# Cross-covariance attention on one core: one late store cut into seven parts instead of four

## The chip, the cores and the metric

The kernel runs on one core of one Trainium2 chip. The metric is device time in microseconds of one execution. Before the change three runs took 128.46 us at the median (128.16 to 128.62). A measurement of this kernel can tell differences of about 0.3% (0.4 us).

## The reference

For each of 8 x 12 = 96 heads, Q, K and V are 512 x 64 in float32. Attention runs over the 64 features and not over the 512 positions:

```
Q_norm = Q / (norm over the 512 positions)      # per feature
K_norm = K / (norm over the 512 positions)
attn = softmax(Q_norm^T K_norm, last axis)      # 64 x 64 for each head
out  = V attn                                   # 512 x 64
```

Inputs and output are 12.58 MB each, so that 37.75 MB are read and 12.58 MB written.

## The kernel before, in words

**Tiling.** Four heads make a unit (`HU` = 4), two units a step (`S` = 12 steps), two steps a group of V (`W` = 6). For a unit, Q and K arrive as 128 partitions x 16 rows of 64; DVE casts them side by side to bfloat16 (L212); PE multiplies each 32 x 128 piece by itself, so that one 128 x 128 sum holds q.q, q.k and k.k (`grams`, L232). The diagonals give the norms (`squares`, `sums`, `powers`), the q.k block is scaled, transposed (`logits`), exponentiated with its row sum (`exps`, L281) and divided (`normalise`, L290). V is cast, transposed by PE (`vtrans`, L301) and copied to SBUF (`vcopy`). `outs` (L318) multiplies it by the normalised weights; `ocopy` copies each quarter of a step's output from PSUM into a tile `so`. When two quarters are there, `store(s, i)` writes the tile to `out`: 128 partitions x 2 runs (the index r = 0 or 1) of 2 KB each, 512 KB. There are 24 such stores, two a step, and 13 buffers for `so`.

**Order of the work.** The order on each engine is fixed when the program is built. A planner (`Order`) is given every piece of work with its engine, its cost, what it needs and a rank, and lists the pieces in order of their planned begin. Loads and stores are pieces of an engine "DMA" and go to SP's queue in the planned order (ACT issues two of the first loads). The plan gives each store one cost and does not look at how `store` divides it, so the diff moves no other piece.

**The end of SP's queue.** After the last loads of V (L196), SP issues the last stores: fourteen whole ones (L206; the last of them is called S14 here), then the divided store FEW = (S - 3, 1), the second half of step 9, and then four whole ones of steps 10 and 11 (L206; T1 to T4 here). FEW leaves in four DMAs: its first half (r = 0) in partitions 0 to 91, 92 to 99 and 100 to 127 (L203, here P1 to P3), and its second half (r = 1) whole (L204, P4). FEW has the same 256 runs of 2 KB as every other store, of which the 92 + 8 + 28 parts hold 128 and P4 the other 128.

**Eight semaphores in turn.** The framework gives the DMAs on the hardware queues eight completion semaphores in turn (DMAHW0 to DMAHW7), and an issue waits until the DMA that had its semaphore before, eight DMAs earlier, has landed. SP executes its list in order, so that while one issue waits, the ones behind it wait too. The ends of the two lists, with the waits, stand in the section on the change.

Of the kernel before, what the change touches and what calls it, by code (L numbers as in the profile page):

```python
# [102 lines left out]
def kernel(  # L103
# [7 lines left out]
    nc = tc.nc  # L111
# [50 lines left out]
    qk32, v32, vb, qkb, gram, scr, kq, n2, r8, kqs, rq, lg, ex, ab, vps, vt, po, so = ({} for _ in range(18))  # L162
# [35 lines left out]
    def store(s, i):  # L198
        o = Of[s // 2, s % 2, i].rearrange("p r (j d) -> p r j d", d=D)
        if (s, i) == FEW:  # L200

            for a, b in ((0, 92), (92, 100), (100, 128)):
                nc.sync.dma_start(out=o[a:b, 0], in_=so[s, i][a:b, 0])  # L203
            nc.sync.dma_start(out=o[:, 1], in_=so[s, i][:, 1])  # L204
            return
        nc.sync.dma_start(out=o, in_=so[s, i])  # L206

# [139 lines left out]
    for i in range(NB["ab"]):  # L347
        a = const.tile([128, HU, 2 * D], BF16, name=f"ab{i}")
# [42 lines left out]
    for u in range(U):  # L391
        s, r = divmod(u, 2)
# [21 lines left out]
    for w in range(W):  # L414
        both = 2 * w >= BOTH
        for r in range(2):
            halves = (0, 1) if (w, r) == (W - 1, 1) else (None,)
            n = 2 * w + r - NB["v"]
# [22 lines left out]
    for s in range(S):  # L441
        for x in range(4):
            i, k = divmod(x, 2)
            n = 4 * s + x - 2
            wait = [("oc", n // 4, n % 4)] if n >= 0 else []
            order = [("ou", s, x - 1) if x else back("ou", s, 1, 3)]
            piece(("ou", s, x), {"PE": 0.5}, [("vc", s // 2, *t) for t in turns(s // 2) if t[0] // 2 == k] + [("nm", s)] + wait, order, R["ou"] + 0.01 * s, outs, s, x)
            n = 2 * s + i - NB["so"]
            free = [("st", n // 2, n % 2)] if k == 0 and n >= 0 else []
            order = [("oc", s, x - 1) if x else back("oc", s, 1, 3)]  # L450
            piece(("oc", s, x), {"ACT": 0.6, "DVE": (0.68, BIAS["oc"])} if s >= BOTH else {"ACT": 0.6}, [("ou", s, x)] + free, order, R["oc"] + 0.01 * s, ocopy, s, x)
        for i in range(2):
            order = [("st", s, 0) if i else back("st", s, 1, 1)]
            piece(("st", s, i), {"DMA": X}, [("oc", s, 2 * i), ("oc", s, 2 * i + 1)], order, v_at(2 * s + i) + ST_LAG, store, s, i)
# [43 lines left out]
```

## Time and profile before

| | |
|---|---|
| median of 3 runs | 128.46 us |
| the profiled execution: its time | 128.35 us |
| the profiled execution: span from first to last instruction | 126.5 us |
| busy: DVE, PE, ACT, POOL | 72%, 62%, 57%, 30% of the span |
| DMA: mean rate over the span | 400 GB/s |
| start of the last compute instruction (ACT copies `so`, L166) | about 115 us |
| issue of the last store | 119.66 us |

How to read it: the span is the profiled execution's own, and its time of 128.35 us has 1.8 us more around it. Every change in the span is set against 128.35 us, which lies 0.11 us under the median of the runs. The "DMA" columns of the profile are a mean over the core's 16 DMA engines. A share a little over 1 occurs, because the records of consecutive packets on one engine overlap by a few ns.

### The profile page before, as it was taken

What the parts mean: (1) busy time and instruction counts of PE and PEld (TensorE: products, weight loads), DVE (VectorE), ACT (ScalarE), POOL (GpSimd) and SP (SyncE); (2) the same over time, 40 slices, a digit from 0 to 9 for tenths busy, and PEclk for the clock granted to TensorE, in tenths of its full rate; (3) what the DMA queues carried; (4) which work ended last, traced back from release to release, by engine and by line L of the source; (5) the groups of instructions that cost most, each with busy time, mean ns of one, the idle gap of its engine ahead of it and who ended that gap; (6) DMA issues with size and microseconds to landing.
All of it is one profiled execution on the core that took longest, in us unless ns stands there. A gap on an engine that the chain in (4) does not pass through costs nothing.

```text
span 126.5 us, 4885 instructions
## 1 busy us (share of the span) xinstructions
PE 78.9 (62%) x2128; PEld 64.2 (51%) x2128; DVE 90.7 (72%) x141; ACT 72.5 (57%) x220; POOL 37.4 (30%) x40
## 2 busy tenths in 40 slices
PE   0065393895964679958583999596676858473000
PEld 0054382784843568747372788484464746352000
DVE  3344749839899499899976798999999799740000
ACT  4000441539789077695883688694758969974000
POOL 4006307300745913043064303133363270300000
PEclk9999999999599555899998559959999999855555
DMA  3999999999999999999999999999999999999993
GB/s 129 408 434 411 427 413 421 413 434 408 430 417 418 409 422 417 398 414 425 422 417 412 418 419 421 416 423 423 401 415 411 402 401 407 400 407 408 405 382 149
DMA packets 15359, 50.64 MB, mean 400 GB/s; under 512 B 1130, under 2 KB 1130, under 8 KB 13930
## 3 DMA queue, kind: packets, MB, share of 16 engines
q1 hardware_dynamic: 15050, 49.29, 96.5%
q10 hardware_dynamic: 288, 1.05, 2.1%
q8 instruction: 16, 0.26, 0.7%
q14 instruction: 5, 0.04, 0.1%
HBM read 37.75 MB, written 12.58 MB: 398 GB/s over the span
## 4 chain that ended last, share of the span: by engine, by line
DVE 34%; DMA 21%; PE 19%; ACT 10%; issue 5%; POOL 2%; SPq 0%; DVEq 0%; ACTq 0%; POOLq 0%
DMA qk<-in_Q_dram 21%; DVE qkb L212 12%; PE gram L232 12%; DVE scr L239 7%; DVE ab L290 5%; ACT so L166 4%; PE po L318 3%; DVE vb L168 3%; ACT ex L281 3%; PE vps L301 3%; DVE n L251 3%; DVE vt L168 2%; ACT vt L166 2%; DVE so L168 1%; POOL kqs L262 1%
## 5 line engine op out<-in xcount | busy, mean ns | idle before, releaser
L232 PE MATMUL gram<-qkb 32*128 32x128 bf16 (+1 forms) x1504 | 36.9, 262 | 20.3 <-DVE qkb L212 7.1
L232 PEld LDWEIGHTS <-qkb 32*128 32x128 bf16 (+1 forms) x1504 | 31.0, 117 | 24.8 <-DVE qkb L212 8.9
L212 DVE CAST qkb<-qk 128x1024 bf16<-128x1024 f32 x48 | 35.3, 758 | 8.4 <-DMA qk<-in_Q_dram 6.8
L170 POOL TENSOR_SCALAR vb<-v 128x1024 bf16<-128x1024 f32 x19 | 22.0, 1169 | 43.9 <-DMA v<-in_V_dram 39.6
L166 ACT COPY so<-po 128x512 f32<-128x512 f32 x45 | 24.8, 593 | 6.6 <-PE po L318 6.5
L166 ACT COPY vt<-vps 128x1024 bf16<-128x1024 bf16 (+1 forms) x18 | 17.8, 987 | 16.5 <-PE vps L301 16.4
L318 PE MATMUL po<-ab,vt 128*64 128x128 bf16 x384 | 20.8, 252 | 5.1 <-ACT so L166 1.7
L301 PE MATMUL vps<-identb,vb 128*128 128x128 bf16 x192 | 18.4, 247 | 6.5 <-POOL vb L170 4.3
L262 POOL TENSOR_TENSOR kqs<-kq,r 64x512 f32<-64x512 f32 x12 | 14.1, 1171 | 26.7 <-ACT r L258 14.0
L239 DVE SCALAR_TENSOR_TENSOR scr<-gram,eye 64x512 f32<-64x512 f32 x24 | 16.5, 687 | 6.0 <-PE gram L232 5.8
L318 PEld LDWEIGHTS <-vt 128*64 128x64 bf16 x384 | 15.2, 127 | 9.4 <-issue 4.8
L301 PEld LDWEIGHTS <-vb 128*128 128x128 bf16 x192 | 13.5, 110 | 10.2 <-POOL vb L170 5.5
L281 ACT ACTIVATE ex<-lg,rq 128x64 f32<-128x64 f32 x48 | 14.5, 322 | 2.5 <-PE lg L275 2.3
L166 ACT COPY kq<-gram 64x512 f32<-64x512 f32 x12 | 7.0, 581 | 13.5 <-DVE scr L239 13.3
L290 DVE TENSOR_TENSOR ab<-ex,rinv 64x256 bf16<-64x256 f32 x24 | 13.4, 556 | 0.6
L281 ACT ACTIVATION_READ_ACCUMULATOR ex<-lg,rq 128x1 f32 x48 | 10.2, 213 | 0.0
L275 PE MATMUL lg<-eye,kqs 64*128 64x64 f32 x48 | 6.4, 258 | 4.3 <-POOL kqs L262 2.6
L251 DVE TENSOR_REDUCE n<-scr 128x8 f32<-128x512 f32 x12 | 8.1, 679 | 0.1
L168 DVE COPY vt<-vps 128x1024 bf16<-128x1024 bf16 (+1 forms) x8 | 7.9, 1020 | 0.1
L168 DVE CAST vb<-v 128x1024 bf16<-128x1024 f32 x5 | 7.0, 1399 | 1.3 <-DMA v<-in_V_dram 1.3
L275 PEld LDWEIGHTS lg<-eye,kqs 64*128 64x128 f32 x48 | 4.5, 156 | 6.1 <-POOL kqs L262 3.3
L287 DVE RECIPROCAL rinv<-esum 128x4 f32<-128x4 f32 x12 | 2.1, 172 | 3.4 <-ACT ex L281 3.2
(17 smaller groups left out, 16.0 us busy)
## 6 DMA issues: line engine op xcount, KB each, us to landing
out_dram<-so SPq DMA_DIRECT2D x23, 512.0 KB, 10.2
v<-in_V_dram SPq DMA_DIRECT2D x11, 1024.0 KB, 17.1
qk<-in_Q_dram SPq DMA_DIRECT2D x8, 1024.0 KB, 17.1
qk<-in_K_dram SPq DMA_DIRECT2D x8, 1024.0 KB, 17.9
qk<-in_Q_dram SPq DMA_DIRECT2D x8, 512.0 KB, 12.2
qk<-in_K_dram SPq DMA_DIRECT2D x6, 512.0 KB, 12.5
qk<-in_K_dram ACTq DMA_DIRECT2D x2, 512.0 KB
v<-in_V_dram SPq DMA_DIRECT2D x2, 512.0 KB
```

Of the source, the lines that this page charges most:

```text
L166: nc.scalar.copy(o, i)
L168: nc.vector.tensor_copy(o, i)
L170: nc.gpsimd.tensor_scalar(out=o, in0=i, scalar1=1.0, scalar2=0.0, op0=ALU.mult, op1=ALU.add)
L212: nc.vector.tensor_copy(qkb[u][:, :, x * D:(x + 1) * D], qk32[s][:, x, r])
L232: nc.tensor.matmul(gram[s][:, h, r, 0], x, x, start=(t == 0), stop=(t == (T if u < WIDE else J) - 1))
L239: nc.vector.scalar_tensor_tensor(out=scr[s][half], in0=gram[s][half, :, :, 0, half].rearrange("p h r d -> p (h r) d"), scalar=1e-20, in1=e ...
L251: nc.vector.tensor_reduce(out=n2[s], in_=scr[s], axis=mybir.AxisListType.X, op=ALU.add)
L262: (nc.vector if eng == "DVE" else nc.gpsimd).tensor_tensor(out=kqs[s][HI], in0=kq[s][HI], in1=r8[s][HI, :, None].to_broadcast([D, 2 * HU, ...
L281: nc.scalar.activation(e[:, h, :], lg[s][:, h, :], AF.Exp, scale=rq[s][:, h:h + 1], accum_out=z[:, h:h + 1])
L290: nc.vector.tensor_tensor(out=a[half, :, half], in0=e[half], in1=ri[half, :, None].to_broadcast([D, HU, D]), op=ALU.mult,)
L301: nc.tensor.transpose(ps[:, c, n, :], vb[w][:, J * c + j].rearrange("p r d -> p (r d)"), identb)
L318: nc.tensor.matmul(po[s, x][e * D:(e + 1) * D, j].rearrange("p r d -> p (r d)"), v, ab[s][:, h, :])
```

## The change

The divided store FEW is cut in another way. Its first half leaves in four DMAs of 92, 24, 7 and 5 partitions, its second half in three of 104, 15 and 9 partitions. Its 256 runs of 2 KB and all values are the same.

```diff
         if (s, i) == FEW:
 
-            for a, b in ((0, 92), (92, 100), (100, 128)):
-                nc.sync.dma_start(out=o[a:b, 0], in_=so[s, i][a:b, 0])
-            nc.sync.dma_start(out=o[:, 1], in_=so[s, i][:, 1])
+            for r, cut in ((0, (92, 24, 7, 5)), (1, (104, 15, 9))):
+                a = 0
+                for n in cut:
+                    nc.sync.dma_start(out=o[a:a + n, r], in_=so[s, i][a:a + n, r])
+                    a += n
             return
         nc.sync.dma_start(out=o, in_=so[s, i])
```

On PE, DVE, ACT and POOL the two programs have the same instructions in the same order. SP has 55 instead of 52 entries. The ends of its two lists, with the semaphores that each issue waits for (S13 and S14 are the last two whole stores ahead of FEW):

```
before                                        after
S13  waits DMAHW6                             S13  waits DMAHW6
S14  waits DMAHW7                             S14  waits DMAHW7
P1   92 partitions     waits DMAHW0           Q1   92 partitions     waits DMAHW0
P2   8 partitions      waits DMAHW1           Q2   24 partitions     waits DMAHW1
P3   28 partitions     waits DMAHW2           Q3   7 partitions      waits DMAHW2
P4   128, second half  waits DMAHW3           Q4   5 partitions      waits DMAHW3
                                              Q5   104, second half  waits DMAHW4
                                              Q6   15, second half   waits DMAHW5
                                              Q7   9, second half    waits DMAHW6
T1   waits DMAHW4                             T1   waits DMAHW7
T2   waits DMAHW5                             T2   waits DMAHW0
T3   waits DMAHW6                             T3   waits DMAHW1
T4   waits DMAHW7                             T4   waits DMAHW2
```

S13, S14, the first part and T1 to T4 also wait for the compute engines that fill their `so` (in before for the DMA semaphores and these together, and so in after).

## The prediction

> **What bounds the kernel now.** I read the page's DMA row first, then SP's issues in order of time, then the DMA columns of the end in stretches of a quarter microsecond.
>
> ```profile
> span 126.5 us, 4885 instructions
> ...
> DMA  3999999999999999999999999999999999999993
> ...
> DMA packets 15359, 50.64 MB, mean 400 GB/s; under 512 B 1130, under 2 KB 1130, under 8 KB 13930
> ...
> q10 hardware_dynamic: 288, 1.05, 2.1%
> ```
>
> The 16 DMA engines are busy from the second slice to the last but one, while no compute engine is over 72%. The last compute work is over by 116 us; behind it lie ten microseconds of stores alone. So the end is set by the DMA engines and by when SP hands them work. Bytes do not change here; what can change is which DMA engine has them, and whether an engine runs dry. SP's issues (start, duration):
>
> ```profile
> 0.74 0.86 SPq L187 DMA_DIRECT2D qk<-in_Q_dram  x2
> ...
> 109.37 0.63 SPq L206 DMA_DIRECT2D out_dram<-so  x1
> 110.66 0.33 SPq L203 DMA_DIRECT2D out_dram<-so  x1
> 111.90 0.29 SPq L203 DMA_DIRECT2D out_dram<-so  x1
> 113.18 0.32 SPq L203 DMA_DIRECT2D out_dram<-so  x1
> 114.49 0.37 SPq L204 DMA_DIRECT2D out_dram<-so  x1
> 115.81 0.39 SPq L206 DMA_DIRECT2D out_dram<-so  x1
> 117.11 0.38 SPq L206 DMA_DIRECT2D out_dram<-so  x1
> 118.38 0.37 SPq L206 DMA_DIRECT2D out_dram<-so  x1
> 119.66 0.37 SPq L206 DMA_DIRECT2D out_dram<-so  x1
> ```
>
> These are S14, P1 to P4 and T1 to T4. They come every 1.24 to 1.32 us although an issue takes only 0.3 to 0.4 us: each waits for the landing of the DMA eight places ahead, and the landings come at the pace of a whole store. A whole store S10 to S14 lands 10.2 us after its issue, T2 to T4 6.0 us after theirs:
>
> ```profile
> DMA to landing us min/median/max: 10.2/10.2/10.2
> ...
> DMA to landing us min/median/max: 6.0/6.0/6.0
> ```
>
> So S14, issued at 109.37, lands at 109.37 + 10.2 = 119.6, and T4, whose issue in before waits for just that landing, goes out at 119.66. T4 lands at 119.66 + 6.0 = 125.7, and 0.8 us later the span ends. Windows of the end (the last two columns are DMA share and GB/s):
>
> ```profile
> 122.00:122.25 0.25, 0.00 (x0) 0.00 (x0) 0.00 (x0) 0.00 (x0) 0.00 (x0) 0.50 1.05 410
> 122.25:122.50 0.25, 0.00 (x0) 0.00 (x0) 0.00 (x0) 0.00 (x0) 0.00 (x0) 0.50 0.93 352
> 122.75:123.00 0.25, 0.00 (x0) 0.00 (x0) 0.00 (x0) 0.00 (x0) 0.00 (x0) 0.50 0.84 328
> 124.75:125.00 0.25, 0.00 (x0) 0.00 (x0) 0.00 (x0) 0.00 (x0) 0.00 (x0) 0.50 0.48 180
> 125.25:125.50 0.25, 0.00 (x0) 0.00 (x0) 0.00 (x0) 0.00 (x0) 0.00 (x0) 0.50 0.02 8
> ```
>
> Up to 122.25 us all 16 engines work (1.05 is a full house). Then three stop (0.84 / 1.05 x 16 = 13 left), 2.5 to 3 us ahead of the last one, which stops between 125.25 and 125.5. The landing at 125.7 follows the last packet by 0.2 to 0.45 us; I take 0.3.
>
> **Two rates.** Between 110 and 122 us the trace has 2556 packets, 172 of them small, all engines busy:
>
> ```profile
> DMA packets 2556, 4.88 MB, mean 407 GB/s; under 512 B 172, under 2 KB 172, under 8 KB 2556
> ```
>
> 2384 runs of 2 KB in 12 us on 16 engines: 12 x 16 / 2384 = 0.0805 us a run on one engine. A whole store gives each engine 256 / 16 = 16 runs, 1.29 us; T1 to T4 together 64 runs, 5.15 us.
>
> **How the parts fall on engines.** The small packets count it: ACT's queue q10 has 288 packets for two DMAs of 128 rows, so 32 small ones, one for each engine of each DMA. The page lists 68 DMAs of 128 partitions beside the three parts; with P4 they are 69, and 69 x 16 = 1104. Of the page's 1130, 26 are left for 92, 8 and 28 partitions. The largest divisors up to 16 are 4, 8 and 14: 26. So P1 gives four engines 23 runs each. For 92, 24, 7, 5, 104, 15 and 9 the same rule gives 4, 12, 7, 5, 13, 15 and 9 engines. If each DMA takes the first engines of one list, the runs of FEW go from 34 (four engines), 11 (four), 10 (six), 8 (two) to 37 (four), 14, 13, 13, 12, 12, 11, 11, 11, 9, 1, 1, 0. The Trainium skill, "DMA: Bandwidth & Descriptors", section "Why a DMA increments its semaphore by 16 and not by 1", states this choice of a divisor and of the lowest-numbered engines; the first agrees with the 26, and the second no view here shows.
>
> **The change part by part.**
>
> *Removed:* 24 runs from three engines, 7 to 9 each, 0.56 to 0.72 us. This is worth nothing unless one of them ends last; three engines already end 2.5 us early, and some ten are still at work at 124.5 us (share 0.73 in the window ahead of it, 0.65 behind). *Added* to the other engines: 1 to 3 runs, 0.08 to 0.24 us (one loses a run).
>
> *Three more issues on SP, about 0.3 us each:* nothing by themselves, since SP idles 0.9 us ahead of each issue.
>
> *The wait that moves:* this is the main term. Q1 to Q4 go out when P1 to P4 did, 110.66 to 114.49, as they wait for the same landings. Q5 now has the place of T1 (115.81), Q6 that of T2, Q7 that of T3 (118.38), and T1 that of T4: it waits for S14 (DMAHW7) and goes out at 119.66 instead of 115.81. What is queued behind it: T2 to T4, which wait for Q1 to Q3. These must land after S14 on the same engines: about 119.7 to 120. T2 goes out at about 120.1, T3 at 120.5, T4 at 120.9 (0.42 us each), far inside the 1.29 us that each store occupies an engine. So only T1 is late.
>
> What does an engine hold from S14's landing until T1's first packet? Parts of FEW alone. S14's landing is told 0.3 us behind its last packet, so the slowest engine is through with S14 at about 119.3, and has up to 14 runs (1.1 us) of FEW, to about 120.4; on the three relieved engines it has one run. The four engines with 37 runs had 2.96 us ahead of them; they can't be slow in S14, or T4 in before would have ended later than 119.3 + 34 x 0.0805 + 5.15 + 0.3 = 127.5. Hence every engine is dry by about 120.5, if T1's packets come later than that.
>
> *The price of T1:* the time from an issue to its first packets, L, with empty rings. No row in the tail shows it, as engines never ran dry there. From below: SP's first load is issued at 0.74, and
>
> ```profile
> 1.50:1.75 0.25, 0.00 (x0) 0.00 (x0) 0.25 (x2) 0.10 (x1) 0.25 (x2) 1.00 0.00 0
> 1.75:2.00 0.25, 0.00 (x0) 0.00 (x0) 0.20 (x1) 0.25 (x1) 0.25 (x1) 1.00 0.61 229
> 2.25:2.50 0.25, 0.00 (x0) 0.00 (x0) 0.00 (x0) 0.25 (x1) 0.00 (x0) 1.00 0.73 262
> 2.50:2.75 0.25, 0.00 (x0) 0.00 (x0) 0.00 (x0) 0.25 (x1) 0.00 (x0) 1.00 1.09 311
> ```
>
> so L is 1.0 us for the first engines, and up to 2.5 - 0.74 = 1.76 for all (there two queues issue at once). From above, in the tail: the three early engines end about 122.4, and began their 64 runs at 117.25, 1.44 us behind T1's issue; L is no longer for them. I take 1.2, between the two nearest rows, 1.0 and 1.44.
>
> *Sum:* 119.66 + 1.2 + 5.15 + 0.3 = 126.3 for the last landing, against 125.7: +0.6 us. With L = 1.0 it is +0.4, with 1.44 +0.85, with 1.76 +1.2. The profiled execution goes from 128.35 to 128.95; the median lies 0.11 above it: 129.1.
>
> For L the Trainium skill, "DMA: Bandwidth & Descriptors", section "Latency and other measured facts", gives about 600 ns to the first byte of such a queue. The trace's 1.0 is longer; by the page's figure T1 would cost nothing, and the sum would be 0.0 by it (the four engines' 37 runs aside).
>
> **Rivals.**
>
> 1. *Not slower: T1 is in time.* Place: T1's first packet at 119.66 + L. Before, the last engine must have begun T1 by 125.7 - 0.3 - 5.15 = 120.25. If L is under 0.6 us, no dry time is left and the balance of runs decides: at best the last engine is among the relieved, and the gain ends at the next one, about 0.2 us, 128.2 to 128.4. For it: the first load's L has a cold start in it. Against: 1.0 us is the only empty-ring row.
> 2. *The four engines with 37 runs decide.* L is 0.6 to 0.9, and one of these four ends last now: 3 runs and 3 small packets more, +0.3 us: 128.75. For it: P1 gave them 23 runs at one stroke. Against: the same L.
> 3. *Longer start.* L is 1.5 to 1.8 on half of the engines as in the first microseconds, or the issues T2 to T4 wait too: +0.9 to +1.2, 129.4 to 129.7. Against: 1.44 in the tail.
> 4. *The parts fall otherwise* (7 or 5 partitions on one engine, say). T1's wait stays, and so does the time, 129.1; only the small packets show it.
>
> **Chances.** Forecast 0.62 (rival 4, with the same time, included), rival 3 0.15, rival 2 0.15, rival 1 0.08. The range takes in rivals 2 and 3: 128.6 to 129.7. Under 0.3%, 0.4 us, a measurement can't tell from no change. From 128.46 that is 128.85: most of the forecast (L from 1.0) is over it, rival 3 as well, rival 2 under it. Slower 0.80, same 0.16, faster 0.04.
>
> **What would show it.** In the profile of the changed kernel: SP issues T1 at 119.6 to 119.7, T2 to T4 within 1.3 us behind it; the windows show the DMA share fall well under 1 between about 119.5 and 121, rise to 1.05 again, and fall steeply at the end, all engines within some 0.3 us, at 125.8 to 126.2; small packets 1104 - 16 + 65 = 1153. I am wrong if the share has no hole there (rival 1), or if T1 is issued before S14 lands.

## The result, and the profile after

The changed kernel takes 129.14 us at the median of 4 runs (129.09 to 129.43), the kernel before 128.41 in the same four rounds. The ratio is 1.0063, 95% interval 1.0039 to 1.0087: slower by 0.6%, 0.73 us. The profiled execution, 129.43 us with a span of 127.62, is the longest of the four. (In a later set one execution of a kernel with eight parts took 287.3 us, with PE busy for 270 us instead of 79; it is left out of the medians and the table.) In the traces SP has 73 DMA issues instead of 70, and every other engine as many instructions as before.

The page of the changed kernel, the rows on DMA:

```profile
span 127.6 us, 4888 instructions
...
DMA  3999999999999999999999999999999999999695
...
DMA packets 15382, 50.64 MB, mean 397 GB/s; under 512 B 1153, under 2 KB 1153, under 8 KB 13953
```

The row of slices, which in the kernel before is full (9) up to the last slice, now has a 6 in the slice from 118.0 to 121.2 us, and behind it a full slice and a half-full one. The small packets are 1153, the number worked out from 4, 12, 7, 5, 13, 15 and 9 engines.

SP's issues around it (start, duration, each from a stretch of its own):

```profile
110.95 7.95 SPq L205 DMA_DIRECT2D out_dram<-so  x7
119.97 0.40 SPq L208 DMA_DIRECT2D out_dram<-so  x1
120.47 0.41 SPq L208 DMA_DIRECT2D out_dram<-so  x1
120.98 0.70 SPq L208 DMA_DIRECT2D out_dram<-so  x1
121.78 1.10 SPq L208 DMA_DIRECT2D out_dram<-so  x1
```

The seven parts take the places from 110.95 to 118.90. T1 goes out at 119.97, where T4 did before; in this execution S14 landed at 119.90 by the semaphore records, 0.3 us later than in the profile before. The windows (last two columns: DMA share, GB/s):

```profile
119.50:119.75 0.25, 0.00 (x0) 0.00 (x0) 0.00 (x0) 0.00 (x0) 0.00 (x0) 0.50 0.57 213
120.00:120.25 0.25, 0.00 (x0) 0.00 (x0) 0.00 (x0) 0.00 (x0) 0.00 (x0) 0.50 0.25 90
120.50:120.75 0.25, 0.00 (x0) 0.00 (x0) 0.00 (x0) 0.00 (x0) 0.00 (x0) 0.50 0.00 0
120.75:121.00 0.25, 0.00 (x0) 0.00 (x0) 0.00 (x0) 0.00 (x0) 0.00 (x0) 0.50 0.41 164
121.00:121.25 0.25, 0.00 (x0) 0.00 (x0) 0.00 (x0) 0.00 (x0) 0.00 (x0) 0.50 1.03 401
125.75:126.00 0.25, 0.00 (x0) 0.00 (x0) 0.00 (x0) 0.00 (x0) 0.00 (x0) 0.50 1.03 401
126.00:126.25 0.25, 0.00 (x0) 0.00 (x0) 0.00 (x0) 0.00 (x0) 0.00 (x0) 0.50 0.27 90
126.25:126.50 0.25, 0.00 (x0) 0.00 (x0) 0.00 (x0) 0.00 (x0) 0.00 (x0) 0.50 0.00 0
```

The engines run out of work one after another; between 120.5 and 120.75 not one moves any data. All start again between 120.89 and 121.07 (packet records), 0.92 to 1.09 us after T1's issue began, and all end between 126.0 and 126.2. The last landing is at 126.54. How SP waits for landings at the end of the program, in the kernel before (us in total, times, longest):

```profile
SPq L493 <- DMA out_dram<-so: 5.5, 5, 1.2
```

The same row of the changed kernel:

```profile
SPq L495 <- DMA out_dram<-so: 3.7, 1, 3.7
```

The program ends with five waits for the eight semaphores, each for two semaphores, in a fixed order. Before, each was ended by a landing: the first by P4's, and the last four by those of T1 to T4, which held a semaphore of each. After, T4 holds a semaphore of the first one, and the other four waits, already met, are gone through behind its landing. From last landing to end of span it was 0.83 us and is now 1.08.

### The profile page after: what moved, and what is told of

Its sections match the earlier page's. It is cut to its first block, busy times and chain, and to the rows that moved or that the text cites. A ratio compares the mean times of both kernels' runs of the same rounds, so it can differ in the third digit from the quotient of the medians.

```text
span 127.6 us, 4888 instructions
## 1 busy us (share of the span) xinstructions
PE 79.2 (62%) x2128; PEld 64.2 (50%) x2128; DVE 93.2 (73%) x141; ACT 72.2 (57%) x220; POOL 36.3 (28%) x40
## 2 busy tenths in 40 slices
DMA packets 15382, 50.64 MB, mean 397 GB/s; under 512 B 1153, under 2 KB 1153, under 8 KB 13953
## 4 chain that ended last, share of the span: by engine, by line
DVE 31%; DMA 27%; PE 17%; ACT 10%; issue 2%; POOL 2%; DVEq 0%; POOLq 0%
DMA qk<-in_Q_dram 19%; DVE qkb L214 12%; PE gram L234 9%; DMA qk<-in_K_dram 8%; DVE scr L241 6%; PE vps L303 5%; DVE ab L292 5%; ACT vt L166 4%; DVE vb L168 3%; ACT so L166 3%; PE po L320 2%; ACT ex L283 2%; DVE n L253 2%; DVE vt L168 1%; DVE so L168 1%
## 5 line engine op out<-in xcount | busy, mean ns | idle before, releaser
L234 PE MATMUL gram<-qkb 32*128 32x128 bf16 (+1 forms) x1504 | 35.1, 256 | 22.2 <-DVE qkb L214 9.4
L234 PEld LDWEIGHTS <-qkb 32*128 32x128 bf16 (+1 forms) x1504 | 29.7, 114 | 26.7 <-DVE qkb L214 12.1
L214 DVE CAST qkb<-qk 128x1024 bf16<-128x1024 f32 x48 | 36.6, 785 | 8.5 <-DMA qk<-in_Q_dram 7.1
L170 POOL TENSOR_SCALAR vb<-v 128x1024 bf16<-128x1024 f32 x19 | 21.2, 1125 | 46.2 <-DMA v<-in_V_dram 40.0
L303 PE MATMUL vps<-identb,vb 128*128 128x128 bf16 x192 | 19.9, 261 | 5.4 <-POOL vb L170 3.7
L303 PEld LDWEIGHTS <-vb 128*128 128x128 bf16 x192 | 14.6, 116 | 9.3 <-POOL vb L170 5.0
L292 DVE TENSOR_TENSOR ab<-ex,rinv 64x256 bf16<-64x256 f32 x24 | 14.1, 589 | 0.6
L168 DVE CAST vb<-v 128x1024 bf16<-128x1024 f32 x5 | 7.5, 1491 | 1.3 <-DMA v<-in_V_dram 1.2
```

What stands on the lines that cost most here:

```text
L168: nc.vector.tensor_copy(o, i)
L170: nc.gpsimd.tensor_scalar(out=o, in0=i, scalar1=1.0, scalar2=0.0, op0=ALU.mult, op1=ALU.add)
L214: nc.vector.tensor_copy(qkb[u][:, :, x * D:(x + 1) * D], qk32[s][:, x, r])
L234: nc.tensor.matmul(gram[s][:, h, r, 0], x, x, start=(t == 0), stop=(t == (T if u < WIDE else J) - 1))
L292: nc.vector.tensor_tensor(out=a[half, :, half], in0=e[half], in1=ri[half, :, None].to_broadcast([D, HU, D]), op=ALU.mult,)
L303: nc.tensor.transpose(ps[:, c, n, :], vb[w][:, J * c + j].rearrange("p r d -> p (r d)"), identb)
```

## Experiments

The theories: **W**, T1 is eight places behind S14, waits for its landing, and the rings run dry; **B**, the shares of the engines cost the time; **C**, three more DMAs cost by themselves. Edits are those of the divided store; "cut" is the list of partitions of the first and the second half. All figures worked out from the profiles, with the medians, stand in the table behind the experiments.

### Seven parts, shares as before

```diff
-cut (92, 24, 7, 5), (104, 15, 9)
+cut (92, 8, 14, 14), (64, 32, 32)
```

> Seven parts with every DMA engine's share of the divided store as it was with four parts (92, 8, 14, 14 and 64, 32, 32 partitions: 4, 8, 14, 14, 16, 16, 16 engines). Theory W (the wait: T1 is eight places behind S14, waits for its landing, and all engines run dry until its packets come): a hole in the DMA share of about 1 us after S14's landing, 129.0 to 129.3 us, as with the change. Theory B (balance: the change lost because it put more runs on engines that end late): no loss, 128.3 to 128.6. Theory C (three more DMAs cost by themselves, by their issue and their completion packets, 0.2 us each): 129.0, but without a hole.

Measured: 129.27 us, ratio 1.0062 (1.0049 to 1.0074). Its windows:

```profile
119.75:120.00 0.25, 0.00 (x0) 0.00 (x0) 0.00 (x0) 0.00 (x0) 0.00 (x0) 0.50 0.51 189
120.25:120.50 0.25, 0.00 (x0) 0.00 (x0) 0.00 (x0) 0.00 (x0) 0.00 (x0) 0.50 0.05 16
120.50:120.75 0.25, 0.00 (x0) 0.00 (x0) 0.00 (x0) 0.00 (x0) 0.00 (x0) 0.50 0.37 147
120.75:121.00 0.25, 0.00 (x0) 0.00 (x0) 0.00 (x0) 0.00 (x0) 0.00 (x0) 0.50 1.05 410
```

The same hole, with every engine's share as it was. B falls: the whole loss is there without the new shares.

### Six parts, shares as before

```diff
+cut (92, 8, 28), (64, 32, 32)
```

> Six parts, shares of the engines as with four parts. Theory W: T1 waits for S13, whose landing comes 1.3 us ahead of S14's, so its packets are there at about 119.3, when the late engines still hold S14 and parts of the divided store; only the early engines run dry, and they have time. The data end as before; 128.4 to 128.7 (the upper end if the last store's semaphore is among the first in the final list of waits, so that more waits follow the last landing). Theory C: two of three steps, 128.8 to 128.9. Theory B: 128.4.

Measured: 128.62 us, ratio 1.0011 (1.0002 to 1.0019). T1 goes out at 118.39, and between 119.5 and 121 us the share is full:

```profile
118.39 0.40 SPq L208 DMA_DIRECT2D out_dram<-so  x1
```

```profile
119.00:119.50 0.50, 0.00 (x0) 0.00 (x0) 0.00 (x0) 0.00 (x0) 0.00 (x0) 0.50 0.87 332
119.50:120.00 0.50, 0.00 (x0) 0.00 (x0) 0.00 (x0) 0.00 (x0) 0.00 (x0) 0.50 1.05 398
120.00:120.50 0.50, 0.00 (x0) 0.00 (x0) 0.00 (x0) 0.00 (x0) 0.00 (x0) 0.50 1.05 410
120.50:121.00 0.50, 0.00 (x0) 0.00 (x0) 0.00 (x0) 0.00 (x0) 0.00 (x0) 0.50 1.03 401
```

Some engines run dry for a while (0.87); the last landing comes 6.19 us after S14's, 0.09 later than before. The loss is not so much a DMA: it steps up between six parts and seven, as W has it.

### Four parts, shares about those of the change

```diff
+cut (92, 36), (117, 11)
```

> Four parts (92, 36 and 117, 11 partitions: 4, 12, 13, 11 engines) that give the engines nearly the shares of the change: 38 runs on four engines, 13 on seven, 12 and 9 on one each, none on three. T1 to T4 are issued as before. Theory W: no hole; the data end 0 to 0.35 us later, by up to four runs on the fullest engines, 128.4 to 128.8. Theory B: the whole loss, 129.0 to 129.2. Theory C: 128.4.

Measured: 128.61 us, ratio 1.0013 (1.0004 to 1.0022). There is no hole:

```profile
119.50:120.00 0.50, 0.00 (x0) 0.00 (x0) 0.00 (x0) 0.00 (x0) 0.00 (x0) 0.50 1.09 422
120.00:120.50 0.50, 0.00 (x0) 0.00 (x0) 0.00 (x0) 0.00 (x0) 0.00 (x0) 0.50 1.06 410
120.50:121.00 0.50, 0.00 (x0) 0.00 (x0) 0.00 (x0) 0.00 (x0) 0.00 (x0) 0.50 1.05 410
```

The shares alone cost 0.13 us; from S14's landing to the last one it takes 0.2 us longer than before. The expectation has the count wrong: by its own numbers of engines the four fullest have 23 + 3 + 9 + 1 = 36 runs and not 38, two more than before and one fewer than with the change, while three others go from 10 to 13.

### Seven parts, three of them behind T4

Ahead of T1 go 92, 24, 104 and 15 partitions; 7, 5 and 9 are issued behind T4.

> The seven parts of the change, but only four of them (92, 24, 104 and 15 partitions) ahead of T1; the other three (7, 5 and 9) are issued behind T4. T1 to T4 then wait for S11 to S14 as before. Theory W: no hole; the four fullest engines end three runs later, 128.5 to 128.8. Theories B and C: 129.0 to 129.2, as both the shares and the number of DMAs are those of the change.

Measured: 129.19 us, ratio 1.006 (1.0046 to 1.0074): W's number missed, B's and C's met. The mechanism is another one, though. There is no hole:

```profile
119.50:120.00 0.50, 0.00 (x0) 0.00 (x0) 0.00 (x0) 0.00 (x0) 0.00 (x0) 0.50 1.07 410
120.00:120.50 0.50, 0.00 (x0) 0.00 (x0) 0.00 (x0) 0.00 (x0) 0.00 (x0) 0.50 1.04 401
120.50:121.00 0.50, 0.00 (x0) 0.00 (x0) 0.00 (x0) 0.00 (x0) 0.00 (x0) 0.50 1.03 401
```

T4 lands at 125.86, 6.02 us after S14, where it was 6.10 before. Then the last of the three small parts lands at 126.26, 0.40 us behind T4 (semaphore records), and the final waits add 0.26. In the profiles that makes 0.58 us of the 0.71 between the medians; the rest is within the 0.35 us by which S14's landing varies from one profile to the next. A median that fits a theory does not yet speak for it; here the edit brought costs of its own, and W's estimate had left both out.

### T1 ahead of the seventh part

As the change, but T1 is issued between the sixth and the seventh part. The number of DMAs, their sizes, the shares and T4's semaphore are those of the change; nothing stands behind T4.

> The seven parts of the change with their shares, but T1 is issued ahead of the seventh part, so that it waits for S13 and not for S14; the rest of SP's list is as with the change, and nothing is behind T4. Theory W (T1 waits for S14's landing and the engines run dry): T1 goes out at 118.4, no hole for the late engines. What is left is three runs more on the four fullest engines (about 0.25 us) and about 0.2 us of final waits after the last landing, since T4's semaphore is the first in the list of final waits, as with the change: 128.6 to 128.9. Theory B (shares) and theory C (number of DMAs): 129.1 to 129.3, as both are those of the change.

Measured: 128.99 us, ratio 1.0046 (1.0033 to 1.0059), 0.1 over W's range and under that of B and C. T1 goes out at 118.61 and T2 at 120.21:

```profile
119.50:120.00 0.50, 0.00 (x0) 0.00 (x0) 0.00 (x0) 0.00 (x0) 0.00 (x0) 0.50 1.01 389
120.50:121.00 0.50, 0.00 (x0) 0.00 (x0) 0.00 (x0) 0.00 (x0) 0.00 (x0) 0.50 0.92 348
121.00:121.50 0.50, 0.00 (x0) 0.00 (x0) 0.00 (x0) 0.00 (x0) 0.00 (x0) 0.50 0.92 356
```

The hole is gone but for some engines that are through with T1 and wait for T2 (0.92). The last landing comes 6.31 us after S14's, with the change 6.64. Taking the wait away gives 0.33 us there and not the whole loss: 0.21 us by the landing, which the hole had covered, and 0.25 us of final waits stay. The 0.21 is put down to the three more runs on the fullest engines; what speaks for it stands under "Shares" below.

### Eight parts, twice

```diff
+cut (92, 8, 14, 14), (32, 32, 32, 32)
```

> Eight parts, shares of the engines as with four. T1 waits for the first part, which lands within 0.3 us of S14. Theory W: the hole of seven parts, hardly longer: 129.1 to 129.4. Theory C (each further DMA costs 0.2 us): 129.4 to 129.6. Theory B: 128.4.

Measured: 129.66 us (median of three runs), ratio 1.0095 (1.008 to 1.0109), 0.3 over W's range and 0.1 over C's. Reading T1's place again, W should have said that the eighth part is what S14's landing releases, and T1 comes one issue behind it. So once more, with that put into numbers:

> Eight parts once more, for an undisturbed profile. Theory W, with what seven and twelve parts showed (the last landing came 6.56 us after the issue of T1 in each): the eighth part is issued on S14's landing, T1 one issue (about 0.42 us) behind it, and the last landing 6.5 to 6.6 us after that; landing to end of span about 1.0 us; 129.6 to 129.8 us. If the cost were one of the further DMA on the engines, T1 would be issued as with seven parts and the packets would end later after it.

Measured: 129.64 us (two runs), ratio 1.0091 (1.0074 to 1.0109). SP's issues:

```profile
119.69 0.32 SPq L205 DMA_DIRECT2D out_dram<-so  x1
120.12 0.40 SPq L208 DMA_DIRECT2D out_dram<-so  x1
```

T1 goes out 0.43 us behind the eighth part, and the last landing is 6.61 us after it. The added cost of the eighth part is T1's later issue.

### Twelve parts

```diff
+cut (92, 8, 14, 14), (16, 16, 16, 16, 16, 16, 16, 16)
```

> Twelve parts (92, 8, 14, 14 and eight times 16 partitions), shares of the engines as with four. T4 has the last semaphore in the list of final waits again. Theory W: a hole as with seven parts or up to 0.3 us longer, as T1 waits for the fifth part; from the last landing to the span's end 0.8 us as before, not 1.0: 129.0 to 129.4. Theory C: 130.0 or more. If the final waits are no cost of their own, landing to end stays at 1.0.

Measured: 131.18 us, ratio 1.0213 (1.02 to 1.0227), far over W's range; C's "130.0 or more" is met. The issues:

```profile
119.57 2.17 SPq L205 DMA_DIRECT2D out_dram<-so  x5
121.85 0.40 SPq L208 DMA_DIRECT2D out_dram<-so  x1
```

S14's landing releases the eighth part at 119.57, four more follow, the last three of them 0.46 us apart, and T1 goes out at 121.85. Until T1's packets come the engines have only these small parts: in the half microseconds from 119.5 to 122.5 the DMA share is 0.06 to 0.32. The last landing is 6.57 us after T1. So it is W with a size that was wrong by four issues, the same slip as with eight parts. The part of the expectation on final waits holds: with T4 on the last semaphore, 0.84 us from landing to end.

### Five parts

```diff
+cut (92, 8, 28), (64, 64)
```

> Five parts (92, 8, 28 and 64, 64 partitions), shares of the engines as with four. T1 waits for S12, so there is no hole. T4's semaphore stands in the third of the five final waits, so that two waits of about 0.065 us follow the last landing. If the final waits are a cost of their own: landing to end of span 0.95 to 0.98 us, between 0.83 with four parts and 1.03 with seven, and 128.5 to 128.65. If not: 0.83, and 128.45.

Measured: 128.57 us, ratio 1.0005 (0.9996 to 1.0014); landing to end 0.94 us, 0.01 under the expected range and 0.11 over the 0.83 that it would be if the waits cost nothing. The ratio alone can't tell 0.1 us from nothing; the profile's 0.94 can, since the five profiles of kernels with T4 on the last wait all have 0.83 or 0.84.

### Fewer runs on the fullest engines

```diff
+cut (76, 52), (64, 64)    # less_on_four
+cut (68, 60), (64, 64)    # still_less_on_four
```

> Four parts (76, 52 and 64, 64 partitions: 4, 13, 16, 16 engines): 31 runs on the four fullest engines in place of 34, 12 on nine, 8 on three. T1 to T4 as before. If the fullest engine sets the end, as the run with 38 runs suggests (0.13 us for four more), three fewer give 0.0 to 0.15 us, until the others with one or two runs more set it: 128.3 to 128.5. If shares don't matter at all: 128.45.

> Four parts (68, 60 and 64, 64 partitions: 4, 15, 16, 16 engines): 29 runs on the four fullest engines, 12 on eleven, 8 on one. T1 to T4 as before. If the fullest engine sets the end: 0.05 to 0.2 us less than before until the next engines set it, 128.25 to 128.4. If the next engines already set it: 128.4 to 128.6.

Measured: 128.35 us, ratio 0.9993 (0.9983 to 1.0002), and 128.55, ratio 1.0003 (0.9994 to 1.0012). (The run "with 38 runs" is the one that has 36.) The first is undecided. The second missed its "fullest engine" range and lies in the other one: with 29 runs on four engines, others set the end. No version was found that beats the kernel before.

### All of them side by side

S14's landing and the last landing are read from the semaphore records of the profiled executions, the rest from SP's issues and the span (us).

| kernel | T1's issue | S14 landing to last landing | T1's issue to last landing | last landing to end | median |
|---|---|---|---|---|---|
| before, four parts | 115.81 | 6.10 | 9.89 | 0.83 | 128.4 to 128.5 |
| four, shares about as after | 115.84 | 6.31 | 10.10 | 0.84 | 128.61 |
| less on four | 115.80 | 6.14 | 9.93 | 0.84 | 128.35 |
| still less on four | 116.03 | 6.12 | 9.89 | 0.84 | 128.55 |
| five parts | 117.29 | 6.26 | 8.75 | 0.94 | 128.57 |
| six parts | 118.39 | 6.19 | 7.40 | 1.02 | 128.62 |
| T1 ahead of last part | 118.61 | 6.31 | 7.52 | 1.08 | 128.99 |
| three behind T4 | 116.04 | 6.42 | 10.21 | 1.09 | 129.19 |
| **the change** | 119.97 | 6.64 | 6.57 | 1.08 | 129.14 |
| seven, shares as before | 119.74 | 6.63 | 6.56 | 1.08 | 129.27 |
| eight parts (second profile) | 120.12 | 7.05 | 6.61 | 1.11 | 129.64 |
| twelve parts | 121.85 | 8.86 | 6.57 | 0.84 | 131.18 |

From seven parts on, the last landing follows T1's issue by 6.56 to 6.61 us, whatever the parts and shares are: from there on T1's issue sets the end. Where it is issued earlier, the last landing follows S14's by 6.1 to 6.4. The last column but one moves by 0.05 to 0.08 us a step with the place of T4's semaphore: last of the five waits (0.83), third (0.94), second (1.02), first (1.08).

## Why the prediction was right

**T1's wait: shown.** It was the main term, and its sign, place and window came as written (all 0.3 us later in the profiled execution, as S14's landing was). It is in the profile after (T1 at T4's old place, an empty window, all engines ending together), and the seven-part kernel with the old shares reproduces it. T1 ahead of the last part removes it, with what was left named above.

**Its size.** Predicted from T1's issue to the last landing: 1.2 + 5.15 + 0.3 = 6.65 us; measured 6.57. L was 0.92 to 1.09 in place of 1.2, near the first load's 1.0 (the other bound, 1.44, was only an upper one), and the last landing came 0.34 us behind the last packet. Of the +0.6 us, the profiles give 6.64 - 6.10 = 0.54 from S14's landing on. The Trainium skill's 600 ns to the first byte ("DMA: Bandwidth & Descriptors", "Latency and other measured facts") is shorter than the 0.92 measured here from the start of T1's issue. The passage does not say where it counts from: from the end of that issue, which took 0.40 us, the first packet came 0.52 us later. The sum counts from the start, where L was over 0.6, so rival 1 had no ground.

**What was left out.** The "0.8 us" behind the last landing was taken as fixed. It grew by 0.25, because T4 moved to a semaphore that the program's end waits for first. So the profiles give 0.54 + 0.25 = 0.79 us, against 0.73 between the medians and a forecast of +0.6. That 129.1 came within 0.04 us of the measured 129.14 is in part luck: of the missing 0.25 us, 0.06 was made up by an L that was too long, and most of the rest by rounding (129.06 to 129.1) and by differences of some 0.05 us between medians and single profiles. In the profiled execution S14 landed 0.3 us later as well, 0.54 + 0.25 + 0.30 = 1.09, which is its 127.62 - 126.53. Between all profiled executions but the one of 287.3 us S14's landing lies between 119.55 and 119.90; the runs don't say why.

**T2 to T4** were to go out within 1.3 us behind T1. They took 1.8, as an issue behind another took 0.5 to 0.8 us; this sign failed. It cost nothing: T4 went out at 121.78, some 3 us before the engines were through with T1 to T3 (three stores of 1.29 us from 120.9 on).

**Shares.** Removing runs from three engines was priced at nothing, adding up to three at 0.08 to 0.24. Alone, nearly these shares cost 0.13 us in the median and 0.21 in the landing; beside the hole they cost nothing that the runs show, with 129.14 us with them and 129.27 without. They come back when the hole goes (T1 ahead of the seventh part: 0.21 again). The semaphore records name no engine, but the landings fit one of the four with the part of 92 partitions: in the kernel before, the last of that part's four landings (119.68) is 23 runs, 1.85 us, behind a landing of S14 at 117.83, and the last landings of the later parts and of T1 to T4 follow it as one engine's would, T1's to T4's 1.27 to 1.30 us apart. With 34 runs the last of T4's 16 landings is 0.22 us behind the next, with 36 and 37 (T1 ahead) 0.28 and 0.29, with 29 only 0.03. With 31 it gained nothing, since in that profile this engine was through with S14 0.27 us later; single profiles can't price three runs (0.24 us). That the named engines are the lowest-numbered ones was not tried; the count of engines was right to the packet.

**Rival 2** (37 runs decide, +0.3 us) is what T1 ahead of the last part points to, with 0.21 us in the landing; in the changed kernel the hole hides it. **Rival 3** (a start of 1.5 us and more) did not come. **Rival 4** does not fit the 1153 small packets, which are the predicted number.

## What to carry to other kernels

With a fixed number of DMAs in flight, what counts is the bytes in flight: seven small DMAs of 512 KB in all fill the places of seven whole stores, the next whole store is issued too late, and the engines run dry until its first packets reach them. Ask of a split first which later issue it pushes behind which landing, then what it does to the balance. At a program's end look also at the order in which the last semaphores are waited for: the last landing should belong to the last wait.

## What the runs showed of the hardware

- With the engines idle, the first packets of the changed kernel's T1 came 0.92 to 1.09 us after the start of its issue, engine by engine. In the kernels with seven (old shares), eight and twelve parts T1's very first packet came 0.91 to 0.92 us after the issue's start; in all four it came 0.52 us after the issue's end.
- Waits that were already met still took about 0.063 us each at the end of SP's list, four of them 0.25.
- In the kernel with three parts behind T4, the last completion packets of T4 and of the three parts stand at 125.42, 125.50, 125.59 and 125.68 us, 0.086 apart, their last landings at 125.86, 125.91, 126.08 and 126.26. What makes the landings fall behind was not tried.
- Issues on SP whose waits are already met followed each other at 0.42 to 0.51 us at first (T1 to T3 of the changed kernel: 0.50 and 0.51), but T4's came 0.79 us behind T3's and itself took 1.10 us. What makes the later ones slower was not tried.
